# One-hot index tiles built on ScalarE, routing begun between the queries, tile stores on ScalarE's queue, and routing spread over more blocks

## The chip, the cores and the metric

The kernel runs on one core of one Trainium2 chip. The metric is the device time of one launch in microseconds. Below, PE is TensorE, DVE is VectorE, ACT is ScalarE, POOL is GpSimd, and SP is SyncE, which only issues transfers here.

## The reference

Two layers run on 256 tokens and 256 context tokens of width 1024. Each layer has a mixer (four kinds of attention and retention) and then a feed-forward part called PEER, which the change is about. PEER looks up 16 experts per head and token among 16384, by two top-16 lists of 128 keys each:

```python
def one_block(xt):                                   # 128 tokens
    q = (xt @ w_q).reshape(PEER_BLOCK, PEER_HEADS, 2, PEER_DK // 2)
    s = jnp.einsum('thpd,hpkd->thpk', q, keys).astype(jnp.float32)
    s1, i1 = lax.top_k(s[:, :, 0], PEER_TOPK)
    s2, i2 = lax.top_k(s[:, :, 1], PEER_TOPK)
    ...
    top_s, top_pos = lax.top_k(cand, PEER_TOPK)      # cand: all 256 sums of s1 and s2
    eidx = jnp.take_along_axis(cand_idx, top_pos, axis=-1)
    g = jax.nn.softmax(top_s, axis=-1)
    act = jax.nn.gelu(jnp.einsum('td,thkd->thk', xt, u[eidx]).astype(jnp.float32), approximate=False)
    return jnp.einsum('thk,thkd->td', (g * act).astype(xt.dtype), v[eidx])
```

Layer 0 does this for both streams (four tiles of 128 tokens), layer 1 for the 256 tokens alone (two tiles).

## The kernel before, in words

PEER is computed densely for most tiles: the Gelu of *all* 16384 expert rows of `u` with all tokens, times a weight matrix G that is zero except at the chosen experts, times all of `v`. In layer 0 one tile is done sparsely instead (POOL gathers its rows, DVE multiplies them, line 919), three densely; in layer 1 both are dense.

The stages of PEER in a layer are:

1. `qT`: eight query heads, each a product with one 128x1024 block of `wq`, copied by ACT (line 953).
2. `peer_u`: 128 blocks of `u`. For a block SP loads `raw` (three buffers), ACT rounds it to `hi` (line 154), DVE takes the rest as `lo` (line 157; five buffers each of `hi` and `lo`, `NW`), PE does 24 matmuls into a PSUM bank `H` (lines 360 to 362), ACT takes the Gelu into `ast` (line 1145), and every two or four blocks SP stores it to `act_d` (line 1147).
3. `peer_v`: 128 blocks of `v`, for which SP loads G and the stored Gelus back.

Between the blocks of `peer_u` stands the routing of the tiles, as a list of tasks with costs written by hand; it is shared out over the first `P - NT` blocks (`NT` = 16), the rest being the tail, which `peer_v` weaves with its first loads. For a tile the tasks are:

- eight `score` tasks: PE makes the scores of four heads (`scp`, line 980), DVE finds the two top-16 lists by MAX8, FIND_INDEX8 and MATCH_REPLACE8 (lines 985 to 990);
- `lists`, `cand`, the second top-16 and the look-ups, again small DVE operations (lines 1006 to 1060);
- for a dense tile 16 tasks `hot` with their PE part `eight`, here together one "hot". A hot makes G for eight tokens: DVE compares indices with a ramp to get the one-hots `a` (line 1093, 128x2048), multiplies half of them by the weights into `bhl` (line 1095, twice 128x1024), PE multiplies the other half with these (16 small matmuls `gps`, lines 1106 and 1107), ACT copies the result to `gst` (line 1109, twice), and after each second hot SP stores it to `g_d` (line 1112).

A scheduler sets the order within each engine's queue at build time; each engine then works strictly in that order. In the trace `peer_u` of layer 0 runs from about 650 to 1308 us, that of layer 1 from about 2203 to 2609 us. "Hot stretch" below is the time from the first to the 15th hot of a dense tile: three in layer 0, two in layer 1. What lies between two hot stretches is a gap, in which DVE does the scores and lists of the next tile; what lies before the first is the start.

Of the kernel before, what the change touches and what calls it, by code (L numbers as in the profile page):

```python
# [8 lines left out]
F32 = mybir.dt.float32  # L9
F32R = mybir.dt.float32r  # L10
BF = mybir.dt.bfloat16
F16 = mybir.dt.float16
U32 = mybir.dt.uint32
AF = mybir.ActivationFunctionType
OP = mybir.AluOpType
# [4 lines left out]
P = 128  # L20
# [4 lines left out]
NEG = -1e30  # L25
X0 = 256
NW = 5
NT = 16
KEEP = 4
LEAD = 2  # L30
SP = 1
# [82 lines left out]
def hybrid_peer(ctx, tc, resin, cvec, modw, modb, nw, win, uq, uk, uv, colw, nab, retl, gnw,  # L114
                wbr, wo, wq, keys, ub, vb, urow, fnw, consts, rconsts, rope, out):
    nc = tc.nc
    pe, dve, act, pool, sync = nc.tensor, nc.vector, nc.scalar, nc.gpsimd, nc.sync
# [15 lines left out]
    def ps_mm(name="mm"):  # L133
        return ps.tile([P, 512], F32, tag="mm", bufs=3, name=name)
# [25 lines left out]
    def next_w(src, after=None):  # L160
        raw = tb.tile([P, 1024], F32, tag="raw", bufs=3, name="raw")
        sync.dma_start(raw, src)
        return split_w(raw, after)
# [201 lines left out]
    act_d = [dr.tile([64, P, 2, 512 - SP * P], F32, name="act_d"), dr.tile([32, P, 4, 256], F32, name="act_d")]  # L365
    g_d = dr.tile([32, P, P, 16], F32, name="g_d")
# [565 lines left out]
    def peer_u(l, hT, rp, ap_, pre, kp_, normed, xrow, vps):  # L932
# [9 lines left out]
        up2 = rp  # L942
        qT = up2.tile([P, 8, n], F32, name="qT")
        kT = up2.tile([P, 8, P], F32, name="kT")
        sync.dma_start(kT, keys[l])
        for h in range(8):
            if h in pre:
                pt, w = pre[h]
                xt_mm(pt[:, X0:], w, hT, X0, 512)
            else:  # L950
                pt = ps_mm("wq")
                xt_mm(pt[:, :n], next_w(wq[l, h], normed if h in (4, 5) else None), hT, tA, 512)
            act.activation(qT[:, h], pt[:, :n], AF.Copy)
        tasks = []

        def add(cost, f):
# [3 lines left out]
        iota = C["iota"]  # L960
        T = {}

        def route(tt):
# [36 lines left out]
            add(200, lists)  # L1000

            def cand(h4):
                cd = up2.tile([P, 4, 256], F32, tag="cand", bufs=2, name="cand")
                T[tt, "cand"] = cd
                v = v16()[:, h4:h4 + 4]
                dve.tensor_tensor(cd.rearrange("p q (a b) -> p q a b", a=16),
                                  v[:, :, 0, :, None].to_broadcast([P, 4, 16, 16]),
                                  v[:, :, 1, None, :].to_broadcast([P, 4, 16, 16]), op=OP.add)
# [34 lines left out]
            add(1500, weights)  # L1043
            for f in range(2):
                def look(f=f):
                    oh = up2.tile([P, 8, 16, 16], BF, tag="cand", bufs=2, name="oh16")
                    ab = T[tt, "abf"][:, f].rearrange("p (h k) -> p h k", h=8)
                    dve.tensor_tensor(oh, ab[:, :, None, :].to_broadcast([P, 8, 16, 16]),
                                      ib16[:, None].to_broadcast([P, 8, 16, 16]), op=OP.is_equal)
                    o = oh.rearrange("p h a (k c) -> p (h a) k c", c=2)  # L1050
                    iv = T[tt, "if"][:, f].rearrange("p h a c -> p (h a) c")
                    dve.tensor_tensor(o, o, iv[:, :, None, :].to_broadcast([P, P, 8, 2]), op=OP.mult)
                    for m in (8, 4, 2):
                        dve.tensor_tensor(oh[:, :, :m], oh[:, :, :m], oh[:, :, m:2 * m], op=OP.add)
                    dve.tensor_tensor(T[tt, "wn"][:, f].rearrange("p (h k) -> p h k", h=8),
                                      oh[:, :, 0], oh[:, :, 1], op=OP.add)
                add(4000, look)

            def look2():
                if tt not in dense:  # L1060
                    wn = T[tt, "wn"]
                    spw["idx"] = kp_.tile([P, P], U32, name="idx")
                    spw["wgt"] = kp_.tile([P, P], F32, name="wgt")
                    dve.scalar_tensor_tensor(wn[:, 0], wn[:, 0], float(P), wn[:, 1], op0=OP.mult, op1=OP.add)
                    dve.tensor_copy(spw["idx"], wn[:, 0])
                    dve.tensor_copy(spw["wgt"], wn[:, 2])
                    return
                tp = ps_o("idxT")
                for q in range(3):
                    pe.transpose(tp[:, q * P:(q + 1) * P], T[tt, "wn"][:, q], ident)  # L1070
                ix = up2.tile([P, 16, 4, 8], F16, tag="ixT", bufs=2, name="ixT")
                tq = tp[:, :384].rearrange("p (q c t) -> p q c t", q=3, t=8)
                act.activation(ix[:, :, 0], tq[:, 0], AF.Copy)
                act.activation(ix[:, :, 1], tq[:, 1], AF.Copy)
                act.activation(ix[:, :, 2], tq[:, 2], AF.Copy, scale=GS)
                dve.scalar_tensor_tensor(ix[:, :, 3], tq[:, 2], GS, ix[:, :, 2], op0=OP.mult, op1=OP.subtract)
                T[tt, "ix"] = ix
# [3 lines left out]
            for c in range(8):  # L1081
                def gsub(c=c):
                    T[tt, "stage"] = up2.tile([P, P, 16], F32, tag="gst", bufs=2, name="gst")
                add(0, gsub)
                for j in range(2):
                    def hot(c=c, j=j):
                        ix = T[tt, "ix"]
                        cur = [ix[:, c * 2 + j, q:q + 2].rearrange("p q (g t) -> p (q g) t", t=2)[:, :, None, :]
                               .to_broadcast([P, 8, P, 2]) for q in (0, 2)]
                        irep = irep2[:, None].to_broadcast([P, 8, P, 2])  # L1090
                        a = up2.tile([P, 8, P, 2], F16, tag="a12", bufs=2, name="a12")
                        bb = up2.tile([P, 8, P, 2], F16, tag="bhl", bufs=2, name="bhl")
                        dve.tensor_tensor(a, irep, cur[0], op=OP.is_equal)
                        for q in range(2):
                            dve.tensor_tensor(bb[:, q * 4:q * 4 + 4], a[:, :4], cur[1][:, q * 4:q * 4 + 4], op=OP.mult)
                        T[tt, "hot", c, j] = a[:, 4:], bb[:, :4], bb[:, 4:], T[tt, "stage"]

                    def eight(c=c, j=j):
                        a2, bh, bl, stage = T.pop((tt, "hot", c, j))
                        for q in range(2):  # L1100
                            gp = ps_s("gps")
                            for i in range(4):
                                t = q * 4 + i
                                o = gp[:, i * P:(i + 1) * P]
                                at = a2[:, t // 2, :, t % 2]
                                pe.matmul(o, at, bh[:, t // 2, :, t % 2], start=True, stop=False)
                                pe.matmul(o, at, bl[:, t // 2, :, t % 2], start=False, stop=True)
                            tc0 = j * 8 + q * 4
                            act.activation(stage[:, :, tc0:tc0 + 4],
                                           gp.rearrange("p (t i) -> p i t", t=4), AF.Copy)  # L1110
                        if j == 1:
                            sync.dma_start(g_d[tt * 8 + c], stage)

                    add(2800, hot)
                    if "late" in T:
                        add(0, T.pop("late"))
                    T["late"] = eight

        irep2 = up2.tile([P, P, 2], F16, name="irep2")
# [8 lines left out]
        add(0, T.pop("late"))  # L1128
        na = 4 if n == 256 else 2
        total = sum(c for c, _ in tasks)  # L1130
        ti, done = 0, 0.0
        stage, keep = {}, {}
        gen = iter(())

        def block(e):
            w = next_w(ub[l, e])
            pt = ps_mm("H")
            xt_mm(pt[:, :nd], w, hT, tD, 512)
            i, j = divmod(e, na)
            if j == 0:  # L1140
                if is_kept(l, i):
                    stage[0] = keep[i] = kp_.tile([P, na, nd], F32, name=f"keep{i}")
                else:
                    stage[0] = ap_.tile([P, na, nd], F32, tag="ast", bufs=2, name="ast")
            act.activation(stage[0][:, j], pt[:, :nd], AF.Gelu)  # L1145
            if j == na - 1 and i not in keep:
                sync.dma_start(act_d[l][i], stage[0])

        lead = sum(c for c, _ in tasks[:first])
        e0 = 15 if first else 0  # L1150
# [8 lines left out]

        for e in range(P - NT):  # L1160
            if e < e0:
# [7 lines left out]
                continue  # L1169
            share = (e + 1 - e0) / (P - NT - 2.0 - e0)  # L1170
            while ti < len(tasks) and done <= lead + (total - lead) * share:
                c, f = tasks[ti]
# [9 lines left out]
        def tail(i):  # L1182
            for e in range(P - NT + i * NT // 4, P - NT + (i + 1) * NT // 4):
                block(e)
                sparse_step()
# [316 lines left out]
```

## Time and profile before

| | before |
|---|---|
| median of 3 runs | 2960.09 us (2955.0 to 2961.21) |
| profiled execution: own time, span | 2968.41 us, 2966.6 us |
| granted clock, mean | 0.988 of full |
| PE busy | 2876.2 us, 97% |
| DVE busy | 2289.3 us, 77% |
| ACT busy | 1298.6 us, 44% |
| POOL busy | 514.1 us, 17% |
| `hi` on ACT (line 154) | 676 of 1060 ns |
| `lo` on DVE (line 157) | 680 of 1226 ns |

PE is nearly always busy over the span as a whole, and ACT less than half of the time. These are means over the mixer, `peer_u` and `peer_v`, which have different limits; the change touches `peer_u` alone, about 1064 us of the span.

### The profile page before, as it was taken

The page shows a single profiled execution, that of the slowest core. Times are in us where ns is not written, and L with a number is a line of the kernel's source. Part 1 is how long each engine was busy: PE and PEld are TensorE (multiplying, and loading weights), DVE is VectorE, ACT ScalarE, POOL GpSimd, SP SyncE. Part 2 cuts the span into 40 slices and gives each one's busy share as a digit, 9 for nine tenths or more (in the row PEclk, how much of TensorE's full clock was granted, in tenths as well). Part 3 has the DMA queues.
Part 4 walks back from the last instruction along what each step waited for, and adds up shares of the span by engine and source line. Part 5 has one row for each costly group of instructions (what it writes and reads, how often), then busy time and mean ns, then how long its engine had stood idle before and what let it go on. Part 6 is the DMA issues. An engine that isn't in the chain of part 4 may idle for free.

```text
span 2966.6 us, 45423 instructions
## 1 busy us (share of the span) xinstructions
PE 2876.2 (97%) x17323; PEld 2525.1 (85%) x17323; DVE 2289.3 (77%) x3933; ACT 1298.6 (44%) x1907; POOL 514.1 (17%) x378
## 2 busy tenths in 40 slices
PE   8999999998999999999999999999999999999998
PEld 6877767788999999998888888887989999988887
DVE  7778784558999899668888787687668797566666
ACT  7234443543343434333333334455554545544443
POOL 0300111101231323235534340101100000000000
PEclk9999999999999999999999999999999999999999
DMA  7354432536697978999999995564556868888885
GB/s 256 115 161 127 154 99 80 162 114 196 218 344 250 327 280 305 358 388 361 381 371 370 367 333 161 168 214 150 168 174 202 275 200 277 300 297 283 277 274 150
DMA packets 242074, 718.34 MB, mean 242 GB/s; under 512 B 24384, under 2 KB 68544, under 8 KB 236736
## 3 DMA queue, kind: packets, MB, share of 16 engines
q1 hardware_dynamic: 204704, 580.69, 58.0%
q0 software_dynamic: 36864, 134.23, 12.6%
q8 instruction: 135, 2.21, 0.3%
q14 instruction: 83, 0.68, 0.1%
q10 hardware_dynamic: 288, 0.52, 0.0%
HBM read 633.56 MB, written 81.79 MB: 241 GB/s over the span
## 4 chain that ended last, share of the span: by engine, by line
PE 72%; DVE 13%; DMA 8%; ACT 3%; issue 3%; POOL 0%; SPq 0%; ACTq 0%; POOLq 0%; DVEq 0%
PE va L1228 29%; PE H L360 6%; PE H L362 6%; PE H L361 6%; DMA raw<-in_ub_dram 4%; PE proj L360 4%; PE proj L361 4%; PE proj L362 4%; DVE lo L157 3%; DMA mraw<-in_modw_dram 2%; DVE macc L252 2%; DVE gat L919 1%; ACT hi L154 1%; PE sc L466 1%; PE ptp L486 1%
## 5 line engine op out<-in xcount | busy, mean ns | idle before, releaser
L154 ACT ACTIVATE hi<-raw 128x1024 fp32r<-128x1024 f32 x676 | 715.8, 1060 | 1257.7 <-DMA raw<-in_ub_dram 301.0
L157 DVE TENSOR_TENSOR lo<-raw,hi 128x1024 fp32r<-128x1024 f32 x680 | 832.8, 1226 | 505.9 <-ACT hi L154 502.0
L360 PE MATMUL H<-h2h,hi 128*128 128x384 f32 (+1 forms) x2048 | 648.7, 317 | 12.0 <-ACT ast L1145 12.0
L362 PE MATMUL H<-h2h,lo 128*128 128x384 f32 (+1 forms) x2048 | 638.4, 313 | 3.2 <-DVE lo L157 3.2
L361 PE MATMUL H<-h2l,hi 128*128 128x384 f32 (+1 forms) x2048 | 639.1, 312 | 0.0
L360 PEld LDWEIGHTS H<-h2h,hi 128*128 128x128 f32 x2048 | 388.9, 190 | 17.3 <-ACT ast L1145 15.5
L1228 PE MATMUL va<-hi,wh 128*128 128x512 f32 x1280 | 397.9, 389 | 0.4 <-ACT keep L1145 0.4
L1228 PE MATMUL va<-lo,wh 128*128 128x512 f32 x1280 | 397.6, 389 | 0.0
L1228 PE MATMUL va<-hi,wl 128*128 128x512 f32 x1280 | 397.3, 389 | 0.0
L362 PEld LDWEIGHTS H<-h2h,lo 128*128 128x128 f32 x2048 | 388.5, 190 | 5.1 <-DVE lo L157 4.6
L361 PEld LDWEIGHTS H<-h2l,hi 128*128 128x128 f32 x2048 | 389.3, 190 | 0.1
L360 PE MATMUL proj<-hh,hi 128*128 128x256 f32 (+1 forms) x808 | 283.7, 353 | 4.4 <-ACT k_t L555 1.8
L1228 PEld LDWEIGHTS va<-hi,wh 128*128 128x128 f32 x1280 | 240.0, 188 | 50.8 <-ACT keep L1145 0.8
L1228 PEld LDWEIGHTS va<-lo,wh 128*128 128x128 f32 x1280 | 240.3, 188 | 49.9
L1228 PEld LDWEIGHTS va<-hi,wl 128*128 128x128 f32 x1280 | 240.3, 188 | 49.7
L361 PE MATMUL proj<-hl,hi 128*128 128x256 f32 (+1 forms) x808 | 278.0, 345 | 0.5 <-DVE rs L296 0.4
L362 PE MATMUL proj<-hh,lo 128*128 128x256 f32 (+1 forms) x808 | 277.7, 344 | 0.0
L909 POOL DMA_INDIRECT gat<-in_urow_dram,idx x128 | 177.4, 1386 | 518.5 <-DVE gat L919 332.0
L909 POOL DMA_INDIRECT gat<-in_vb_dram,idx x128 | 213.2, 1665 | 268.6 <-DVE spacc L929 247.3
L252 DVE SCALAR_TENSOR_TENSOR macc<-mraw,cs,macc 128x512 f32<-128x512 f32 x224 | 169.3, 792 | 37.7 <-DMA mraw<-in_modw_dram 34.6
L360 PEld LDWEIGHTS proj<-hh,hi 128*128 128x128 f32 x808 | 154.5, 192 | 28.0 <-issue 4.2
L299 POOL TENSOR_TENSOR rs<-rs,mhalf 128x1 f32<-128x1 f32 x16 | 11.0, 687 | 956.6 <-DVE rs L296 919.6
(300 smaller groups left out, 4307.2 us busy)
## 6 DMA issues: line engine op xcount, KB each, us to landing
raw<-in_ub_dram SPq DMA_DIRECT2D x256, 512.0 KB
raw<-in_vb_dram SPq DMA_DIRECT2D x256, 512.0 KB
raw<-in_win_dram SPq DMA_DIRECT2D x112, 512.0 KB
mraw<-in_modw_dram SPq DMA_DIRECT2D x160, 256.0 KB
g_d<-gst SPq DMA_DIRECT2D x40, 1024.0 KB
act_d<-ast SPq DMA_DIRECT2D x64, 384.0 KB
a<-act_d SPq DMA_DIRECT2D x64, 384.0 KB
G<-g_d SPq DMA_DIRECT2D x32, 768.0 KB
```

The lines of the kernel that those rows point to most:

```text
L154: act.activation(hi, raw, AF.Copy)
L157: lo_turn["last"] = dve.tensor_tensor(lo, raw, hi.bitcast(F32), op=OP.subtract)
L252: dve.scalar_tensor_tensor(acc[st], w, cs[:, k, st:st + 1], acc[st], op0=OP.mult, op1=OP.add)
L299: pool.tensor_tensor(r[:, 1:2], r[:, 0:1], mhalf, op=OP.pow)
L360: pe.matmul(o, a, hh[:, k, c0:c1], start=(k == 0), stop=False)
L361: pe.matmul(o, a, hl[:, k, c0:c1], start=False, stop=False)
L362: pe.matmul(o, b, hh[:, k, c0:c1], start=False, stop=(k == KD - 1))
L466: pe.matmul(sps[hb][:, :n], qf(h, tt), kf(h, n), start=True, stop=True)
L486: pe.transpose(tp[:, c * P:(c + 1) * P], pt[:, c * P:(c + 1) * P], ident)
L909: pool.indirect_dma_start(buf[j], None, urow if j < P else vrow, bass.IndirectOffsetOnAxis(ap=idx[:, k:k + 1], axis=0))
L919: dve.scalar_tensor_tensor(g, g, 1.0, xrow, op0=OP.mult, op1=OP.mult, accum_out=hk[:, 0, k:k + 1])
L1228: pe.matmul(pacc[tt][h], x[:, tsl], y[:, h * 512:(h + 1) * 512], start=(e == 0 and x is wh and y is vh), stop=(e == P - 1 and x is wl))
```

## The change

- **One-hots on ACT.** Of a hot's 16 one-hot columns, the eight that are multiplied by weights now come from ACT: eight `Abs` of (ramp minus index) on 128x128 into `dif`, one `Relu` of 1 minus `dif` on 128x1024 into `one`. DVE's compare `a` shrinks from 128x2048 to 128x1024. ACT copies the negated indices once per tile into `nx`. `dif` has one buffer, `one` two.
- **First scores earlier.** Five tasks of the first tile (`begin`, scores of heads 0 to 3) are issued between query heads 0 to 3 and 4 to 7.
- **Stores on ACT's queue.** The 88 `act_d` and 40 `g_d` stores are issued by ACT instead of SP.
- **Longer routing.** `NT` goes from 16 to 12: tasks are spread over the first 116 blocks instead of 112.
- `cand` and `oh16` get one buffer instead of two.

```diff
-NT = 16
+NT = 12
...
-        for h in range(8):
+        def queries(h):
...
+        for h in range(4):
+            queries(h)
         tasks = []
...
-                cd = up2.tile([P, 4, 256], F32, tag="cand", bufs=2, name="cand")
+                cd = up2.tile([P, 4, 256], F32, tag="cand", bufs=1, name="cand")
...
+                T[tt, "nx"] = up2.tile([P, P], F32, tag="nx", bufs=2, name="nx")
+                act.activation(T[tt, "nx"], tp[:, :P], AF.Copy, scale=-1.0)
...
-                        irep = irep2[:, None].to_broadcast([P, 8, P, 2])
-                        a = up2.tile([P, 8, P, 2], F16, tag="a12", bufs=2, name="a12")
+                        irep = irep2[:, None].to_broadcast([P, 4, P, 2])
+                        a = up2.tile([P, 4, P, 2], F16, tag="a2", bufs=2, name="a2")
                         bb = up2.tile([P, 8, P, 2], F16, tag="bhl", bufs=2, name="bhl")
-                        dve.tensor_tensor(a, irep, cur[0], op=OP.is_equal)
+                        dif = up2.tile([P, 4, P, 2], F16, tag="dif", bufs=1, name="dif")
+                        one = up2.tile([P, 4, P, 2], F16, tag="one", bufs=2, name="one")
+                        nx = T[tt, "nx"]
+                        for t in range(8):
+                            x = c * 16 + j * 8 + t
+                            act.activation(dif[:, t // 2, :, t % 2], iota, AF.Abs, bias=nx[:, x:x + 1])
+                        act.activation(one, dif, AF.Relu, scale=-1.0, bias=1.0)
+                        dve.tensor_tensor(a, irep, cur[0][:, 4:], op=OP.is_equal)
                         for q in range(2):
-                            dve.tensor_tensor(bb[:, q * 4:q * 4 + 4], a[:, :4], cur[1][:, q * 4:q * 4 + 4], op=OP.mult)
-                        T[tt, "hot", c, j] = a[:, 4:], bb[:, :4], bb[:, 4:], T[tt, "stage"]
+                            dve.tensor_tensor(bb[:, q * 4:q * 4 + 4], one, cur[1][:, q * 4:q * 4 + 4], op=OP.mult)
+                        T[tt, "hot", c, j] = a, bb[:, :4], bb[:, 4:], T[tt, "stage"]
...
-                            sync.dma_start(g_d[tt * 8 + c], stage)
+                            act.dma_start(g_d[tt * 8 + c], stage)
...
-        ti, done = 0, 0.0
+        ti, done = 5, 0.0
+        for c, f in tasks[:ti]:
+            f()
+            done += c
+        for h in range(4, 8):
+            queries(h)
...
-                sync.dma_start(act_d[l][i], stage[0])
+                act.dma_start(act_d[l][i], stage[0])
```

The scheduler orders the queues anew. On ACT, at the first hots of layer 0's first dense tile, the order before is:

```order
L1075 ACTIVATE ixT<-idxT 128x16x8
L154 ACTIVATE hi<-raw 128x1024
L1145 ACTIVATE ast<-H 128x384
L154 ACTIVATE hi<-raw 128x1024
L1145 ACTIVATE ast<-H 128x384
L1109 ACTIVATE gst<-gps 128x128x4 x2
L154 ACTIVATE hi<-raw 128x1024
L1145 ACTIVATE ast<-H 128x384
L1109 ACTIVATE gst<-gps 128x128x4 x2
L154 ACTIVATE hi<-raw 128x1024
```

and of the change, at the same place (lines 1104 and 1105 are the new `Abs` and `Relu`, 1122 is `gst`, 1163 `ast`):

```order
L1081 ACTIVATE ixT<-idxT 128x16x8
L1104 ACTIVATE dif<-consts,nx 128x128 x8
L154 ACTIVATE hi<-raw 128x1024
L1105 ACTIVATE one<-dif 128x1024
L1163 ACTIVATE ast<-H 128x384
L1104 ACTIVATE dif<-consts,nx 128x128 x8
L1165 DMA act_d<-ast 128x768
L1105 ACTIVATE one<-dif 128x1024
L1122 ACTIVATE gst<-gps 128x128x4 x2
L1104 ACTIVATE dif<-consts,nx 128x128 x8
L1163 ACTIVATE ast<-H 128x384
L1105 ACTIVATE one<-dif 128x1024
```

Nine new instructions stand in each hot, and the stores stand among `hi`, `ast` and `gst`.

On DVE, in the same hot stretch, the order before is:

```order
L1093 TENSOR_TENSOR a_7296<-irep_5723,ixT 128x2048
L157 TENSOR_TENSOR lo<-raw,hi 128x1024
L1095 TENSOR_TENSOR bhl<-a_7296,ixT 128x1024 x2
L919 SCALAR_TENSOR_TENSOR gat,hk<-gat,xrow 128x1024
L157 TENSOR_TENSOR lo<-raw,hi 128x1024
L1093 TENSOR_TENSOR a_7358<-irep_5723,ixT 128x2048
```

and of the change (989 to 994 are the scores of the next tile):

```order
L1106 TENSOR_TENSOR a_7320<-irep_5595,ixT 128x1024
L989 MAX v_8380<-scp_8382 128x8
L990 MAX_INDEX i_8381<-v_8380,scp_8382 128x8
L1108 TENSOR_TENSOR bhl<-one,ixT 128x1024 x2
L992 MATCH_REPLACE rep<-v_8380,scp_8382 128x128
L989 MAX v_8380<-scp_8382 128x8
L993 MAX v_8380<-rep 128x8
L990 MAX_INDEX i_8381<-v_8380,scp_8382 128x8
L994 MAX_INDEX i_8381<-v_8380,rep 128x8
L1106 TENSOR_TENSOR a_7429<-irep_5595,ixT 128x1024
L1108 TENSOR_TENSOR bhl<-one,ixT 128x1024 x2
```

Before, the next tile's scores stood behind the hots; now about 140 small operations for the next tile stand among the hots of the first hot stretch of each layer.

On PE, within layer 0's fifth query, the eight `scp` matmuls of the first four heads (line 980 before, 984 now) are moved ahead:

```order
 L361 MATMUL wq<-h2l,hi 128x512
 L362 MATMUL wq<-h2h,lo 128x512
+L984 MATMUL scp_5601<-kT,qT 128x128
+L984 MATMUL scp_5602<-kT,qT 128x128
+L984 MATMUL scp_5601<-kT,qT 128x128
+L984 MATMUL scp_5602<-kT,qT 128x128
+L984 MATMUL scp_5601<-kT,qT 128x128
+L984 MATMUL scp_5602<-kT,qT 128x128
 L360 MATMUL wq<-h2h,hi 128x512
```

Before, they stood behind the last matmul of the eighth query. On SP the stores are gone, and 119 loads of `raw` stand in a row where at most a few stood between two stores.

## Rows read from the trace of the kernel before

**Rows 1.** Windows: start:end, length, PE, PEld, DVE, ACT, POOL busy (count), clock, DMA share, GB/s.

```profile
650.20:812.60 162.40, 149.73 (x848) 145.40 (x845) 150.25 (x506) 52.87 (x74) 28.03 (x22) 0.96 0.60 196
812.60:892.10 79.50, 74.95 (x562) 72.37 (x560) 74.14 (x106) 34.98 (x57) 25.09 (x18) 0.98 0.93 338
892.10:975.90 83.80, 81.31 (x487) 78.47 (x484) 81.51 (x256) 28.92 (x45) 17.09 (x15) 1.00 0.73 256
975.90:1061.40 85.50, 81.41 (x594) 78.39 (x591) 78.68 (x137) 36.63 (x60) 26.77 (x18) 0.96 0.92 334
1061.40:1145.60 84.20, 78.66 (x461) 76.42 (x458) 84.15 (x236) 29.04 (x42) 27.75 (x18) 0.98 0.75 261
1145.60:1225.90 80.30, 75.87 (x564) 73.45 (x562) 72.97 (x96) 35.80 (x60) 28.70 (x20) 0.96 0.95 350
1225.90:1308.20 82.30, 81.64 (x474) 80.94 (x473) 49.83 (x64) 30.47 (x45) 25.30 (x20) 1.00 0.97 373
2202.70:2292.10 89.40, 86.50 (x736) 85.23 (x732) 81.52 (x249) 43.20 (x66) 0.00 (x0) 1.00 0.64 200
2292.10:2377.20 85.10, 85.10 (x827) 84.44 (x824) 66.89 (x70) 46.94 (x79) 0.00 (x0) 1.00 0.79 268
2377.20:2467.80 90.60, 90.58 (x791) 89.85 (x789) 83.13 (x251) 45.13 (x71) 0.00 (x0) 1.00 0.65 203
2467.80:2552.80 85.00, 85.00 (x827) 84.37 (x825) 66.41 (x70) 46.60 (x79) 0.00 (x0) 1.00 0.85 289
2552.80:2608.70 55.90, 55.90 (x476) 55.82 (x474) 25.27 (x23) 27.77 (x43) 0.00 (x0) 1.00 0.91 306
```

**Rows 2.** The same stretches, matmuls, weight loads and Gelus of `H` alone.

```profile
892.10:975.90 83.80, 74.28 (x409) 71.45 (x409) 8.60 (x18) 1.00 0.73 256
2377.20:2467.80 90.60, 86.83 (x721) 85.88 (x722) 10.94 (x30) 1.00 0.65 203
```

**Rows 3.** A wait of PE in `peer_u` of layer 0: us in total, times, longest.

```profile
PE H L360 <- ACT ast L1145: 11.2, 7, 4.1
```

**Rows 4.** Chain of waits from 829 to 848 us, DVE's links.

```profile
829.68 1.14 DVE a L1093
830.82 1.14 DVE lo L157
831.95 1.22 DVE bhl L1095 x2
846.29 1.14 DVE gat L919 x2
```

**Rows 5.** ACT's operations: timeline at 870 us, chain at 64 us, and one tile.

```profile
870.64 1.06 ACT L154 ACTIVATE hi<-raw 128x1024 fp32r<-128x1024 f32 x1
871.61 0.47 ACT L1145 ACTIVATE ast<-H 128x384 f32<-128x384 f32 x1
871.98 1.08 ACT L1109 ACTIVATE gst<-gps 128x512 f32<-128x512 f32 x2
63.97 1.17 ACT dec L542 x4
L542 ACT ACTIVATE dec<-rcon,lg x16: 386/388/402, 61.9 to 1855.8; 128x128 f32<-128x128 f32 x16
```

**Rows 6.** The start of layer 0: fourth query on ACT, first score, last waited-for scores.

```profile
627.63 0.58 ACT L953 ACTIVATE qT<-wq 128x512 f32<-128x512 f32 x1
651.30 0.49 DVE L985 MAX8 v<-scp 128x8 f32<-128x128 f32 x2
738.40 2.07 PE L980 MATMUL scp<-kT,qT 64*128 64x128 f32 x8 [7.95 <-DVE rep L988]
```

**Rows 7.** The `act_d` stores on SP, and SP's and ACT's waits (650 to 1308 us).

```profile
L1147 SPq DMA_DIRECT2D act_d<-ast x88: 320/326/2327, 660.3 to 2599.6; - x88
SPq L1147 <- ACT ast L1145: 204.4, 54, 9.5
ACT hi L154 <- DMA raw<-in_ub_dram: 226.2, 70, 10.5
```

More of the change, by code (lines that the diff above doesn't have):

```diff
@@ L1045, in look @@
                 def look(f=f):
-                    oh = up2.tile([P, 8, 16, 16], BF, tag="cand", bufs=2, name="oh16")
+                    oh = up2.tile([P, 8, 16, 16], BF, tag="cand", bufs=1, name="oh16")
                     ab = T[tt, "abf"][:, f].rearrange("p (h k) -> p h k", h=8)
```

## The prediction

> **What bounds the kernel now.** I read the windows first, cut at the first and the 15th hot of each dense tile [rows 1]. Layer 0's `peer_u` is 658.0 us long, its PE is busy for 623.6: the idle 34.4 us are 12.7 in the start, 4.1 to 4.6 in each hot stretch, 2.5 and 5.5 in the gaps, 0.7 in the tail. DVE is full in the gaps (81.51 of 83.80, 84.15 of 84.20) and nearly so in the hot stretches; ACT is at 35 to 37 us of 80. Layer 1's 406.0 us hold 403.1 of PE: 2.9 idle, all in the start. So PE's work, which the change keeps, allows at most some 37 us of gain, and layer 1 has almost none to give. Then the waits: PE waits in layer 0 for `ast`, which empties its banks, 11.2 us in seven waits [rows 3], and 8.0 us once for a score bank that DVE still reads [rows 6]. The chain through a hot stretch alternates between PE and DVE's `a`, `lo`, `bhl` and `gat` at 1.14 to 1.22 us each [rows 4].
>
> **Prices.** DVE pays 1.14 for `lo` and `gat`, 1.14 for `a` and 1.22 for the two `bhl` [rows 4]. The halved `a` is a `bhl` in size: 0.60. A hot thus falls from 2.36 to 1.82, over 80 hots 43 us. Of the 81.51 us in the first gap, 15 `lo`, 16 `gat` and two hots take 40.0; the other 41.5 are 137 small operations, 0.30 each. On ACT `hi` takes 0.97 to the next start, `ast` 0.37, `gst` 0.54 [rows 5]. A `Relu` is as large as `hi`: 1.06. `Abs` on 128x128 with a pointer operand is not in the trace; the nearest is `dec` (line 542) on the same shape, four in 1.17 us, 0.29 each. From above 0.39 bounds it, the duration of one `dec` without overlap; from below 0.13, a quarter of a 512-column `gst`. I take 0.29, as it runs eight in a row. A store costs its queue 0.33 [rows 7]. ACT's part in a hot goes from 1.08 to 1.08 + 8 x 0.29 + 1.06 = 4.5 us, over 80 hots 270 us.
>
> A block of `u` costs PE 74.28/17 = 4.37 us in layer 0, 86.83/30 = 2.89 in layer 1 [rows 2] and a hot 0.94 (what 25 blocks of 2.89 leave of 85.1, in 14 hots). Longer routing moves blocks: I counted in the orders how many stand in each stretch after the change. Before has 32, 14, 17, 15, 17, 14, 19 in layer 0, the change 32.5, 13.5, 19, 14, 19, 15, 15; layer 1 has 29, 25, 30, 25, 19, then 31, 24, 33, 24, 16. Each stretch below is compared with its time of before for the changed number of blocks, at 4.28 us (just under the tail's 81.64/19 = 4.30 [rows 1]) and 2.89; both counts sum to 128, so this price cancels.
>
> **Layer 0.**
> - *Start, 164.5 before.* The fourth query is copied at 627.6, so the first score can begin at 629 instead of 651.3 [rows 6]: 22.3 us earlier. DVE then has six more `lo` and three more `gat` between first score and first hot, 10.3 us. The first hot comes 12 us earlier, after 150.4 us; PE was busy for 149.7 of this stretch, so all of its idle 12.7 goes and there is no more to gain. **-14.1.**
> - *First hot stretch, 77.4 before.* DVE's queue holds 14 hots (25.5), 12 `lo` and 13 `gat` (28.5) and 142 small operations of the next tile (43): **97**, where it was busy for 74. ACT has 112 `Abs`, 14 `Relu`, 28 `gst`, 12 `hi`, 14 `ast`, 14 stores: 32.5 + 14.8 + 15.1 + 11.6 + 5.2 + 4.6 = 84. PE has 73. The queue is in order, so the hots wait behind the scores. **+19.6.** Bounds: 80, if the five buffered `lo` keep PE fed while DVE runs late, and 101, if ACT's 84 does not lie beside it fully.
> - *First gap, 92.4 before.* DVE now has 76 us, PE 19 blocks and a little (83 + 2): 85. **-7.4.**
> - *Second hot stretch, 81.2 before.* PE 75.5, DVE up to 78, ACT 83 by the same sum. PE's idle was 4 in such a stretch, so between 79.5 and 88; I take ACT's 83. **+1.8.**
> - *Second gap, 92.8 before.* DVE falls to 60, since its work was done early; PE 84.5. **-8.3.**
> - *Third hot stretch, 84.6 before.* ACT 85, PE 78: 84. **-0.6.**
> - *Tail, 65.2 before for 15 blocks.* The last `g_d` store and the loads of G now fall into fewer blocks. The DMA share was 0.97 of 82.3; less four blocks of 0.5 MB at 373 GB/s it still needs 74. I take 68, between PE's 65 and this. **+2.8.**
>
> Sum: **-6.2**, from 658 to 652.
>
> **Layer 1.** Start, 95.2 before: I take 1 of the 2.9 idle: 94. First hot stretch, 82.2 before: DVE 14 hots, 22 `lo` and 140 small operations, 25.5 + 25.1 + 42.4 = 93; ACT 95 with 24 `hi` and 24 `ast` of 0.26; PE 83. Two engines at 93 to 95 in strict orders, with no sparse step between: 97 (85 to 101). Gap, 99.3 before: PE 33 blocks and 2: 97. Second hot stretch, 82.1 before: PE 83, ACT 82: 84.5. Tail, 47.2 before for 16 blocks: 51, since the same loads of G come in fewer blocks. Sum **+17.5**: 406 to 423.5. Here no idle PE pays for it: DVE's 43 us were not on the path, ACT's 270 come onto it.
>
> **Stores and buffers.** I price the move of the stores at nothing beyond ACT's 0.33 each. SP waited 204.4 us for `ast` with a store at its head, and ACT 226.2 us for `raw` behind it [rows 7]: it looks as if `raw` would come much earlier. But what counts is PE, and it waited 11.2 us for `ast` [rows 3]; a store that no longer blocks SP can give at most that. The Trainium skill (DMA: Bandwidth & Descriptors, "Issuing engines are not separate DMA queues") says that transfers issued by any engine run on the same 16 DMA engines and interleave, so issuing from another saves only the sequencer's time; by that rule the move takes 128 x 0.33 = 42 us off SP and puts it on ACT, and the loads themselves come no faster; the trace bears it out so far that ACT's 226.2 us of waiting cost PE only 11.2. What waits behind a store on ACT is `hi` and `ast` of the next block; the store follows the `ast` or `gst` that it needs, so its wait is done when it comes up. One `cand` buffer costs nothing: the two uses are in order on DVE.
>
> **Sum.** -6.2 + 17.5 = **+11.3 us** against the profiled execution, whose own time is 2968.4, 8 above the median of the runs; mixer and `peer_v` keep their order. On the median 2960.1: **2971 us**. Its own range is 2966 to 2995: the first hot stretches' bounds give -17 -12 and +4 +4, the tail +6, the others up to +5 each, of which not all fall together; the low end is cut where other cases begin.
>
> **Rivals.**
> 1. *The buffers absorb it: faster.* In both first hot stretches five `hi`/`lo` are ready ahead, 5 x 4.37 = 22 us of PE work in layer 0, 14 in layer 1. If DVE's lateness of 97 - 73 = 24 stays within them and is paid back in the gap (DVE 76 of 85), these stretches are 80 and 86: -17 and -11, and with 4 less in the others 2971 - 32 = 2939. For it: DVE lags PE only within a stretch. Against it: in the hot stretches before, five buffers did not prevent 4 to 5 us of idle with DVE less full, and the gap pays back 9. It decides at a first stretch under about 86 in layer 0.
> 2. *`Abs` does not overlap.* At 0.39 each ACT has 95 in every hot stretch: +11 in the three that ACT sets, +3 in the others, and `hi` comes late, so SP's loads too, which now all stand in a row on three buffers: 2971 + 39 = 3010. For it: `dif` has one buffer, so that `Abs` of the next hot waits for `Relu`. Against it: `dec` ran at 0.29 four times in a row.
> 3. *It cancels.* The start and gaps give 30 us in layer 0; if layer 1's stretch loses only 7 instead of 15 and the tails nothing, the sum is -3: 2957, no difference.
>
> **Chances.** Differences under 0.2% (6 us) are about what a measurement of this kernel cannot tell from none. My forecast (6 to 35 slower) 0.36, rival 2 0.15, cancelling 0.20, rival 1 0.29. So faster 0.29, same 0.20, slower 0.51. For 8 in 10 the range reaches from rival 1's time to rival 2's: 2938 to 3010; below it some of rival 1 is left out, above it some of rival 2.
>
> **What would show it.** The start is right if the first score begins near 629, the 8.0 us wait at line 980 is gone, and the first hot comes near 800. The first hot stretches are right if DVE is over 95% busy there and they are 95 to 100 long; if they are under 86, rival 1 is. ACT's price is right if an `Abs` starts every 0.29 us and ACT sums to 82 to 85 in the hot stretches; rival 2, if it is 95 and PE waits for `ast` and `gst`. The gaps are right if DVE is idle in them and PE is not. The forecast is wrong above all if DVE's work for the next tile, though earlier in the queue, gets done while PE lives from its buffers.

## The result, and the profile after

The change takes 3122.52 us (median of 4 runs, 3114.23 to 3127.66) against 2960.22: a ratio of 1.0543, 95% interval 1.0526 to 1.056. The forecast was 2971, with a range from 2938 to 3010. The sign was right; the size was wrong by an order of magnitude.

The profiled execution has a span of 3112.3 us, 145.7 more than before. On its page PE is busy for 2924.0 us, 47.8 more, though it does the same matmuls; the other 97.9 us are idle time of PE. All of it lies in `peer_u`: from the first to the last `H` matmul layer 0 takes 734.8 us (657.8 before) and layer 1 477.2 (405.8).

The windows of the changed kernel, cut at the same events as [rows 1] (start:end, length, PE, PEld, DVE, ACT, POOL busy, clock, DMA share, GB/s):

```profile
645.20:801.40 156.20, 149.84 (x860) 146.47 (x859) 136.93 (x419) 59.40 (x92) 28.46 (x24) 0.98 0.66 219
801.40:911.10 109.70, 86.08 (x589) 80.46 (x586) 99.06 (x298) 77.45 (x176) 17.01 (x13) 0.88 0.61 212
911.10:1003.50 92.40, 85.69 (x494) 84.84 (x492) 79.18 (x174) 44.64 (x76) 32.33 (x25) 0.94 0.87 310
1003.50:1115.70 112.20, 87.83 (x585) 81.36 (x583) 78.58 (x189) 76.12 (x173) 14.48 (x12) 0.85 0.59 203
1115.70:1203.20 87.50, 84.23 (x493) 83.38 (x491) 58.58 (x80) 44.84 (x78) 30.34 (x24) 0.98 0.91 333
1203.20:1306.30 103.10, 88.65 (x591) 82.66 (x589) 59.01 (x85) 81.23 (x184) 18.77 (x14) 0.88 0.63 221
1306.30:1380.20 73.90, 67.02 (x381) 66.02 (x379) 45.54 (x59) 29.19 (x40) 24.50 (x18) 0.95 0.99 376
2273.30:2364.60 91.30, 91.15 (x781) 90.64 (x780) 77.91 (x209) 51.05 (x90) 0.00 (x0) 1.00 0.67 208
2364.60:2486.10 121.50, 100.18 (x838) 95.55 (x835) 97.33 (x275) 87.37 (x195) 0.00 (x0) 0.89 0.52 174
2486.10:2585.70 99.60, 96.81 (x829) 96.16 (x827) 50.98 (x49) 71.09 (x131) 0.00 (x0) 1.00 0.73 238
2585.70:2693.20 107.50, 91.90 (x804) 88.52 (x802) 48.68 (x60) 76.72 (x169) 0.00 (x0) 0.94 0.57 196
2693.20:2750.70 57.50, 50.62 (x404) 49.79 (x402) 26.24 (x24) 29.86 (x45) 0.00 (x0) 0.94 0.83 276
```

The loss sits in the five hot stretches: 109.7, 112.2, 103.1, 121.5 and 107.5 us where 97, 83, 84, 97 and 84.5 were forecast, 108.5 us in excess. No engine is full in them. ACT's sums, 76 to 87, are near the forecast ones, but ACT is idle for 22 to 36 us in each: lengths less busy time give 32.3, 36.1, 21.9, 34.1 and 30.8. The third and fifth stretch have no next-tile work on DVE (59.01 and 48.68 busy) and are long all the same. The granted clock is 0.85 to 0.94.

What ACT and PE wait for, first ACT in the first hot stretch (us in total, times, longest), then PE over the whole span, then SP:

```profile
ACT ast L1163 <- PE H L362: 30.1, 12, 8.7
...
PE H L360 <- ACT hi L154: 55.0, 29, 6.6
PE H L362 <- DVE lo L157: 45.7, 32, 6.1
...
SPq L162 <- DVE lo L157: 460.5, 79, 37.2
```

ACT waits for PE and PE for ACT. The third row, of SP from 801 to 1307 us, rules out late loads: for 460.5 us SP waited for `lo` to free a `raw` buffer, so `raw` lay there and `hi` was late. One such place, on ACT's timeline (start, length, what):

```profile
873.98 0.49 ACT L1163 ACTIVATE ast<-H 128x384 f32<-128x384 f32 x1 [1.27 <-PE H L362]
874.37 1.05 ACT L1105 ACTIVATE one<-dif 128x1024 f16<-128x1024 f16 x1
874.51 0.33 ACTq L1165 DMA_DIRECT2D act_d<-ast  x1
875.32 1.08 ACT L1122 ACTIVATE gst<-gps 128x512 f32<-128x512 f32 x2
876.27 0.45 ACT L1104 ACTIVATE dif<-consts,nx 128x128 f16<-128x128 f32 x1
876.42 0.33 ACTq L1125 DMA_DIRECT2D g_d<-gst  x1
876.80 2.19 ACT L1104 ACTIVATE dif<-consts,nx 128x128 f16<-128x128 f32 x7
878.86 1.04 ACT L154 ACTIVATE hi<-raw 128x1024 fp32r<-128x1024 f32 x1
```

and what PE and DVE make of it:

```profile
879.95 0.44 PE L360 MATMUL H<-h2h,hi 128*128 128x384 f32 x1 [1.55 <-ACT hi L154]
880.23 0.34 PE L361 MATMUL H<-h2l,hi 128*128 128x384 f32 x1
886.68 0.69 PE L362 MATMUL H<-h2h,lo 128*128 128x384 f32 x1 [6.11 <-DVE lo L157]
...
885.40 1.22 DVE L157 TENSOR_TENSOR lo<-raw,hi 128x1024 fp32r<-128x1024 f32 x1
```

The `hi` of the next block stands *behind* the `ast` of the block that PE is just finishing. So ACT waits for PE; then it does `one`, two `gst` and eight `dif`, 4.9 us after the start of `ast`, before it makes `hi`; then DVE, busy with the next tile, makes `lo` 5.5 us later; and only then can PE go on. Call the number of blocks by which ACT's queue holds `hi` ahead of `ast` the **lead**. Counted from ACT's order, it is 2 to 5 in all hot stretches before. In those of the change it is 0 to 2 after the first few blocks, and 0 at 28 of 92 blocks. Call a block with lead 0 a **place**.

Counted in the trace by blocks, these 28 places hold nearly the whole loss. Between the end of such a block and the end of the next one on PE lie 11.7 us in the mean, with 2.6 us of other ACT work between `ast` and `hi`; behind the other 64 blocks it is 4.0 us. (Some hots stand there too: 1.5 behind a place, 0.6 behind another block, by the forecast under 1 us each.) PE is idle for 112.0 us behind the 28 places and for 2.8 behind the other 64, of 132.4 in the two `peer_u`. In run e5 below, where the lead is 3, the 83 blocks of the hot stretches take 4.6 us each, with 12.9 us of idle time together.

### The profile page after: what moved, and what is told of

It is laid out like the page before. It is cut to its first block, busy times and chain, and to the rows that moved or that the text cites. A ratio compares the mean times of both kernels' runs of the same rounds, so it can differ in the third digit from the quotient of the medians.

```text
span 3112.3 us, 46158 instructions
## 1 busy us (share of the span) xinstructions
PE 2924.0 (94%) x17323; PEld 2561.6 (82%) x17323; DVE 2256.2 (72%) x3933; ACT 1568.2 (50%) x2632; POOL 523.1 (17%) x378
## 4 chain that ended last, share of the span: by engine, by line
PE 69%; DVE 14%; issue 6%; DMA 4%; ACT 4%; POOL 1%; SPq 0%; POOLq 0%; DVEq 0%; ACTq 0%
PE va L1246 28%; PE H L362 6%; PE H L360 6%; PE H L361 6%; DVE lo L157 4%; PE proj L360 4%; PE proj L362 3%; PE proj L361 3%; DMA mraw<-in_modw_dram 1%; ACT hi L154 1%; DVE macc L252 1%; PE sc L466 1%; PE attno L499 1%; POOL gat L909 1%; PE ptp L486 1%
## 5 line engine op out<-in xcount | busy, mean ns | idle before, releaser
L360 PE MATMUL H<-h2h,hi 128*128 128x384 f32 (+1 forms) x2048 | 663.7, 324 | 59.1 <-ACT hi L154 55.0
L362 PE MATMUL H<-h2h,lo 128*128 128x384 f32 (+1 forms) x2048 | 660.8, 323 | 45.7 <-DVE lo L157 45.7
L361 PE MATMUL H<-h2l,hi 128*128 128x384 f32 (+1 forms) x2048 | 655.0, 320 | 0.0
L360 PEld LDWEIGHTS H<-h2h,hi 128*128 128x128 f32 x2048 | 405.2, 198 | 66.9 <-ACT hi L154 61.0
L362 PEld LDWEIGHTS H<-h2h,lo 128*128 128x128 f32 x2048 | 403.8, 197 | 56.0 <-DVE lo L157 55.7
L361 PEld LDWEIGHTS H<-h2l,hi 128*128 128x128 f32 x2048 | 404.3, 197 | 0.1
L909 POOL DMA_INDIRECT gat<-in_vb_dram,idx x128 | 232.2, 1814 | 247.0 <-DVE spacc L929 231.7
L909 POOL DMA_INDIRECT gat<-in_urow_dram,idx x128 | 165.0, 1289 | 611.5 <-DVE gat L919 404.7
L1104 ACT ACTIVATE dif<-consts,nx 128x128 f16<-128x128 f32 x640 | 209.3, 436 | 1.7
L1163 ACT ACTIVATE ast<-H 128x384 f32<-128x384 f32 (+1 forms) x224 | 97.7, 436 | 171.5 <-PE H L362 170.1
```

The costliest lines, as they stand in the source:

```text
L360: pe.matmul(o, a, hh[:, k, c0:c1], start=(k == 0), stop=False)
L361: pe.matmul(o, a, hl[:, k, c0:c1], start=False, stop=False)
L362: pe.matmul(o, b, hh[:, k, c0:c1], start=False, stop=(k == KD - 1))
L909: pool.indirect_dma_start(buf[j], None, urow if j < P else vrow, bass.IndirectOffsetOnAxis(ap=idx[:, k:k + 1], axis=0))
L1104: act.activation(dif[:, t // 2, :, t % 2], iota, AF.Abs, bias=nx[:, x:x + 1])
```

## The experiments

All ratios are to the kernel before, timed on the same chip (medians there 2963 to 2965 us for the runs, 2960 for the change), with 95% intervals. "ACT one-hots" is the number of columns per hot that ACT builds.

| run | ACT one-hots | stores on | lead in hot stretches | next-tile work among hots on DVE | us | ratio |
|---|---|---|---|---|---|---|
| the change | 8 | ACT | mostly 0 to 2 | 142, 79, 0; 140, 0 operations | 3122.5 | 1.0543 (1.0526 to 1.0560) |
| e1 | none | ACT | 2 to 5 | 7 at most | 2947.2 | 0.9935 (0.9918 to 0.9952) |
| e2 | 8 | SP | mostly 1 | 48, 65, 0; 68, 0 | 2990.0 | 1.0080 (1.0064 to 1.0097) |
| e3 | 8 | SP | mostly 1 | 46, 28, 0; 41, 0 | 2987.9 | 1.0075 (1.0058 to 1.0092) |
| e4 | 8 | ACT | 3 | 143, 79, 0; 137, 0 | 3037.6 | 1.0247 (1.0230 to 1.0264) |
| e5 | 8 | ACT | 3 | none | 3000.0 | 1.0122 (1.0105 to 1.0139) |
| e6 | 8 | ACT | 0 to 2 | none | 3127.0 | 1.0556 (1.0536 to 1.0576) |
| e7 | 8 | SP | 3 to 4 | 57, 13, 0; 0, 0 | 2983.5 | 1.0068 (1.0051 to 1.0085) |
| e8 | none | ACT | 3 to 5 | 9 at most | 2956.8 | 0.9979 (0.9964 to 0.9994) |
| e10 | 4 | SP | 3 to 5 | none | 2944.4 | 0.9933 (0.9910 to 0.9956) |
| e11 | none | ACT | 3 to 5 | none | 2947.8 | 0.9945 (0.9925 to 0.9964) |
| e12 | none | SP | 2 to 5 | 9 at most | 2952.0 | 0.9959 (0.9944 to 0.9974) |
| e15 | 4 | ACT | 3 to 4 | 48, 28, 0; 0, 0 | 2970.5 | 1.0019 (1.0008 to 1.0030) |
| e16 | 4 | ACT | 3 to 4 | none | 2968.2 | 1.0014 (1.0002 to 1.0025) |

The semicolon parts layer 0's three hot stretches from layer 1's two. Runs e9, e13 and e14 force places of lead 0 and stand below.

**e1, the change without ACT's one-hots.** DVE's old lines 1093 and 1095 are put back, `nx`, `dif` and `one` are gone.

> The change without ACT's one-hots: DVE compares all 2048 columns again; early scores, stores on ACT's queue, longer routing stay. Theory A (ACT's queue holds hi only 0 to 2 blocks ahead of ast in the hot stretches, so that ACT waits for PE with the next hi behind it, and PE for ACT): here the queue holds hi 3 or more ahead throughout, so 2950 us (2930 to 2970), PE's waits for hi under 5 us. Theory B (ACT's added work is too much in itself, whatever the order): also 2950. Theory C (stores on ACT's queue hold up hi): 3100 (3070 to 3125).

2947.2 us. The rest of the change is a gain of 0.65%; A and B hold, C falls as stated (the lead is 2 to 5, where A had 3 or more).

**e2, the one-hots alone,** in the kernel before.

> The kernel before with ACT's one-hots alone (and one cand buffer). The queue holds hi 1 to 2 blocks ahead of ast in the hot stretches. Theory A: 3100 us (3060 to 3140), hot stretches over 100 us. Theory B: 3110 (3090 to 3140). Theory C: 2970 (2950 to 2990).

2990.0, at the upper end of C's range. The one-hots alone cost 0.8%, not 5%. A's claim that a lead of 1 is enough to lose the time is refuted here, and so is B.

**e3, the stores back on SP.**

```diff
-                            act.dma_start(g_d[tt * 8 + c], stage)
+                            sync.dma_start(g_d[tt * 8 + c], stage)
...
-                act.dma_start(act_d[l][i], stage[0])
+                sync.dma_start(act_d[l][i], stage[0])
```

> The change with the stores back on SP. The queue holds hi 1 block ahead of ast in most of the hot stretches (0 to 2 in the change). Theory A: 3090 us (3050 to 3125), a little less than the change since a lead of 0 is rare. Theory B: 3110 to 3120, less the 128 issues of 0.33 us at most. Theory C: 2970 (2950 to 3000).

2987.9: again in C's range, 135 us below the change. So most of the loss needs both, ACT's one-hots *and* the stores on ACT's queue; e1 has one and e3 the other. But moving them also lets the scheduler order the queues anew: the lead is 1 instead of 0, and 46 operations instead of 142 stand among the first tile's hots. Whether the stores or the order cost the time was to be told next.

**e4, `hi` and `lo` written three blocks ahead,** stores on ACT.

```diff
+AHEAD = 3
...
+        ws = []
...
+        def fetch(e):
+            while len(ws) < min(e + AHEAD, P):
+                ws.append(next_w(ub[l, len(ws)]))
...
-            w = next_w(ub[l, e])
+            fetch(e + 1)
+            w = ws[e]
...
         for e in range(P - NT):
+            fetch(e)
```

> The change with the load, hi and lo of a block written three blocks ahead in the program, so that ACT's queue holds hi 3 blocks ahead of ast in all hot stretches; the work of each engine is the same. Theory A: 2975 us (2940 to 3010), PE's waits for hi and lo under 20 us, hot stretches 85 to 97 us. Theory B: 3100 (3080 to 3130), hot stretches still over 100. Theory C: 3100 too.

3037.6: between both. The third and fifth hot stretch fell from 103.1 and 107.5 to 85.2 and 89.2 us, as A said; those with next-tile work stayed at 109.4, 107.7 and 120.5. There `gst` waited for PE, and PE for `bhl` and `lo`, which stood behind that work on DVE (busy 98.53 of 109.40 in the first). PE's waits over the span, of which A had put those for `hi` and `lo` under 20 us:

```profile
PE H L363 <- DVE lo L158: 36.5, 19, 4.0
PE gps L1120 <- DVE bhl L1109: 21.8, 9, 5.3
```

**e5, e4 and the next tile's scores queued behind the last hot; e6, these scores alone.**

```diff
+                    with tc.issue_after(inst(T["bhl"])) if "bhl" in T else ExitStack():
                         for f in range(2):
...
-                            dve.tensor_tensor(bb[:, q * 4:q * 4 + 4], one, cur[1][:, q * 4:q * 4 + 4], op=OP.mult)
+                            T["bhl"] = dve.tensor_tensor(bb[:, q * 4:q * 4 + 4], one, cur[1][:, q * 4:q * 4 + 4], op=OP.mult)
```

> The change with hi and lo three blocks ahead as before, and the scores of the next tile queued on DVE behind the last hot of the tile before; the stores stay on ACT's queue. Theory O (the order is what costs: next-tile work among the hots on DVE, and hi 0 to 2 blocks ahead on ACT; the scheduler made this order because the stores were on ACT): 2985 us (2965 to 3005), hot stretches as long as ACT's sum, 76 to 83 us in layer 0 and 88 to 92 in layer 1. Theory P (the stores themselves hold up ACT's queue): 3030 (3015 to 3060).

> The change with only the scores queued behind the last hot; hi stays 0 to 2 blocks ahead in the hot stretches, stores on ACT. Theory O: 3060 us (3030 to 3090): all five hot stretches at 100 to 108 us, like the third and fifth of the change, which have no next-tile work in them. Theory P: 3100 or more (3090 to 3130). If next-tile work alone were the cause: 2985.

e5 takes 3000.0, as O said and P did not. e6 takes 3127.0: above O's range and inside P's, so neither theory holds as it was stated. O was wrong that next-tile work costs time where the lead is 0 to 2; P is wrong that the stores explain the loss by themselves, since e5 has them too. Between the two edits only the three blocks ahead differ (`raw`, `hi` and `lo`), with the same stores and the same work on each engine: **127 us for the lead**. In the traces `peer_u` is 137 us shorter, and the stretch between the layers 11 longer. The next-tile work is worth 38 us where the lead is 3 (e4 against e5) and nothing where it is 0 to 2 (the change against e6). The windows of the five hot stretches, e5's and then e6's:

```profile
806.80:883.10 76.30, 72.60 (x554) 65.20 (x551) 54.12 (x79) 75.50 (x177) 14.87 (x13) 1.00 0.80 280
988.10:1062.80 74.70, 71.69 (x534) 65.47 (x532) 54.86 (x80) 74.15 (x172) 14.24 (x12) 0.98 0.85 291
1168.50:1243.70 75.20, 68.78 (x525) 62.41 (x522) 55.03 (x80) 74.69 (x177) 14.66 (x13) 1.00 0.82 282
2312.80:2402.90 90.10, 90.10 (x868) 88.58 (x864) 54.90 (x67) 88.00 (x198) 0.00 (x0) 1.00 0.71 240
2503.30:2590.60 87.30, 87.30 (x842) 86.37 (x840) 53.74 (x65) 86.79 (x195) 0.00 (x0) 1.00 0.75 252
...
804.20:905.30 101.10, 87.49 (x588) 81.79 (x586) 61.96 (x101) 81.44 (x185) 19.99 (x15) 0.88 0.70 237
1004.50:1112.30 107.80, 88.99 (x570) 82.38 (x568) 58.83 (x95) 80.22 (x183) 16.22 (x14) 0.87 0.67 222
1212.70:1311.60 98.90, 84.67 (x570) 78.77 (x568) 60.22 (x87) 80.89 (x184) 19.91 (x15) 0.88 0.70 241
2370.90:2486.70 115.80, 98.96 (x826) 95.00 (x824) 52.28 (x64) 87.63 (x196) 0.00 (x0) 0.88 0.56 187
2596.10:2708.70 112.60, 92.63 (x804) 88.65 (x801) 51.88 (x63) 87.67 (x195) 0.00 (x0) 0.94 0.59 197
```

In e5 ACT does what it did in the changed kernel, in 75 to 90 us, and is idle for 2.1 at most. In layer 0 its sum now sets the stretch, as the prediction took it to; in layer 1 PE is full as well (90.10 of 90.10 and 87.30 of 87.30). In e6 ACT has about the same sums and is idle for 18 to 28 us in each.

PE's waits in e6, for comparison with the two rows of the change above:

```profile
PE H L360 <- ACT hi L154: 73.7, 33, 6.7
PE H L362 <- DVE lo L157: 25.0, 38, 2.9
```

**e7, e4 with the stores on SP; e8, the stores alone in the kernel before.**

> The change with hi and lo three blocks ahead and the stores on SP; the scheduler then leaves at most 57 next-tile operations among a tile's hots, against 143. Theory O and theory P both: 2980 us (2960 to 2995), as with the stores on SP alone (2988), the hot stretches being as long as ACT's sum.

> The kernel before with only the stores moved to ACT's queue. Theory O: no harm where ACT has idle time and the order keeps hi 3 or more blocks ahead: 2960 us (2945 to 2968 with before at 2965). Theory P: slower by 20 to 60 us, 2985 to 3025.

2983.5, which both theories gave and which decides nothing between them, and 2956.8, as O said and P did not. The hot stretches of e7 are ACT's nearly from end to end (73 to 87 us of its work in 73 to 89); the first:

```profile
813.60:888.80 75.20, 74.88 (x562) 66.15 (x560) 66.89 (x168) 75.20 (x180) 15.93 (x12) 1.00 0.79 280
```

**e9, no part of the change, but every eighth `hi` put behind the `ast` of the block before it.**

```diff
+            late = e % 8 == 4 and e > 4
+            with tc.issue_after(inst(T["ast"])) if late else ExitStack():
-            w = next_w(ub[l, e])
+                w = next_w(ub[l, e])
```

> The kernel before, without any part of the change, but with hi of every eighth block queued on ACT behind the Gelu (ast) of the block before it: 29 or so places where the queue holds hi no block ahead. Theory O (lead): each place costs PE ast 0.47 + hi 1.06 + lo 1.22 = 2.7 us and some more for the clock, 29 x 3 to 4.5 = 87 to 130: 3050 to 3095 us. If the lead is harmless and only ACT's added work counts: 2964 to 2975.

3001.9 us (1.0131, 1.0104 to 1.0158): 37 us in a kernel that has nothing else of the change. The edit makes 30 places, 15 in each layer, so 1.2 us each, less than half of the low bound. Nothing stands between `ast` and `hi` at these places, where 2.6 us did in the change; PE is idle for 32 us behind the 30. But the rest of the order changed too: 44, 41, 0; 112, 0 next-tile operations stand among the hots, where before has 9 at most. So not all of the 37 us need be the lead's.

**e13 and e14, the same places in e7 and e10:** is it that ACT was full?

> The kernel of e7 (ACT builds eight columns, hi three ahead, stores on SP; ACT busy for 99 to 100% of the hot stretches), with hi of every eighth block queued behind the Gelu of the block before it, as in e9. Theory R (where ACT is full, each wait of ACT for PE adds its whole length to the stretch): more than e9's 37 us over e7, since some 10 of the 29 places lie in hot stretches and cost 4 us or more there: 3055 us (3035 to 3080). If the places cost the same whatever ACT's load: 3020 (3012 to 3030).

> The kernel of e10 (four columns on ACT; ACT busy for 80% of the hot stretches) with the same places. Theory R: ACT has room, so the places cost as in e9: 2944 + 37 = 2981 us (2970 to 2993). If ACT's work itself, full or not, makes the places dear: 3000 or more.

3033.8 (1.0242, 1.0217 to 1.0268), 50 over e7 and between the two ranges on record, and 3025.6 (1.0209, 1.0185 to 1.0232), 81 over e10 and in the range for "ACT's work itself". Theory R falls: ACT with room pays more. What a place costs is not fixed, and how full ACT is does not order it. That ACT's work makes the places dear is not shown either, since the scheduler made a new order in each of these runs: 47, 85, 0; 131, 0 next-tile operations stand among e13's hots and 35, 55, 0; 135, 0 among e14's, against 57 at most in e7 and none in e10. At the places `lo` begins 0.8 us after the end of its `hi` in e9, 1.4 in e13 and 1.9 in e14, the order of the three costs. This points to DVE's queue, but no run holds that queue fixed.

**e10, four columns on ACT, four on DVE;** hi ahead, stores on SP.

```diff
-                        a = up2.tile([P, 4, P, 2], F16, tag="a2", bufs=2, name="a2")
+                        a = up2.tile([P, 6, P, 2], F16, tag="a2", bufs=2, name="a2")
...
-                        for t in range(8):
+                        for t in range(4):
```

> ACT builds four columns of a hot instead of eight, DVE the other four; hi three blocks ahead, stores on SP. If what was left of the loss there (2983 us with eight columns) is ACT's sum in the hot stretches: ACT's part of a hot falls by 4 x 0.29 + 0.5 = 1.7 us, 24 us in each stretch, so that PE bounds them: 2955 us (2940 to 2968). If it is something else, DVE's order say: 2980 (2972 to 2990).

2944.4, 39 below e7, as the forecast for ACT's sum had it. ACT is at 56 to 57 of 68 to 71 us in layer 0's hot stretches, and layer 1's are at PE's 85.1 and 85.0 again.

**e11, e1 with hi ahead; e12, the early scores alone.**

> The change without ACT's one-hots, and hi and lo three blocks ahead. By theory O nothing is to be had, since hi was 3 or more ahead there too: 2946 us (2938 to 2956), as without it (2947).

> The kernel before with the first four heads' scores between the queries alone. If the first score's 22 us come through to the first hot in part, 2955 us (2948 to 2961 with before at 2964); the rest of the 18 us by which the change without one-hots is faster would then be the stores' 7 and the longer routing's few. If the start is bound by PE and not by DVE: 2964.

2947.8 and 2952.0. Where the lead is 2 to 5 already, writing `hi` further ahead gives nothing. The early scores give 12 of e1's 18 us, the stores 7 by e8; the longer routing was not run by itself.

**e15 and e16, e10 with the stores on ACT,** e16 with the scores behind the last hot.

> The kernel of e10 with the stores on ACT's queue. If the stores cost nothing where ACT has room and the order keeps hi three ahead: 2946 us (2938 to 2958). If the stores as such delay ACT: 2965 or more.

> The kernel of e15 (four columns on ACT, hi three ahead, stores on ACT) with the next tile's scores queued behind the last hot, so that DVE's queue holds no next-tile work among the hots, as with the stores on SP (e10, 2944). If that next-tile work is what made e15 26 us longer than e10: 2950 us (2940 to 2958). If stores on ACT's queue cost as such: 2965 or more, as in e15 (2970).

2970.5 and 2968.2: 26 and 24 us over e10. Both lie where the texts on record had put them if stores on ACT cost as such, and the next-tile work does not explain it. What the traces say of it stands under "Open" below.

## Why the prediction was wrong

**What failed** is the step that sums each engine's work in a hot stretch and takes the largest sum, first with "PE has 73. The queue is in order, so the hots wait behind the scores", then "I take ACT's 83". The sums were near: ACT 77.45, 76.12 and 81.23 against 84, 83 and 85, in layer 1 87.37 and 76.72 against 95 and 82, an `Abs` every 0.29 us (seven in 2.06 above). Of the 84, 4.6 were stores; in the rows above the store at 874.51 is issued while `one` runs, so that it took no time from ACT's other work. (PE's price of a hot, 0.94, comes to 0.92 by its own numbers; nothing hangs on it.) So what failed is the overlap, not a price: the step lets three engines work side by side without asking whether they can. What stood in the orders and was not read is which instruction stands before which. Sums bound a stretch only if each engine has something to do while it waits; with the lead at 0 ACT and PE take turns, 112 us of idle PE behind 28 places. In the change the stretches are ACT's sum and 22 to 36 us of waiting. e5 and e7, with the lead at 3, are what the step described.

**The stores,** priced "at nothing beyond ACT's 0.33 each", were the second failure: 135 us by e3. The argument that a store's wait is over when it comes up holds in the change: ACT is idle for `ast <- PE`, not for a store. With the stores moved the scheduler came to another order. In e5 and e6, with the stores on ACT in both, the lead is worth 127 us, so a lead like e6's can account for the 135. Without the one-hots the move gives 0.2% (e8). The Trainium skill (DMA: Bandwidth & Descriptors, "Issuing engines are not separate DMA queues") has it that issuing from several engines saves only the sequencer's time, and e8's 0.2% doesn't contradict that. It says nothing of what else moves.

**The rivals.** The second named part of it (`hi` late, while ACT is filled) but with the wrong cause: `Abs` does overlap, and `raw` was not late. The first, that buffers absorb it, needs a lead that the queue didn't have.

**What held.** The first score came at 623.4 instead of 651.3, the first hot at 801.4 where "near 800" stood, and e12 shows the early scores alone. The start itself took 156.2 us instead of 150.4, but `peer_u` began 5 us earlier. DVE fell in the second gap to 58.58 (60). The 8.0 us wait at the score bank shrank to 2.5. The gaps were 92.4 and 87.5 for 85 and 84.5, the tails 73.9 and 57.5 for 68 and 51, layer 1's start and gap 91.3 and 99.6 for 94 and 97: 23 us too low together. And the core of the forecast, that ACT's work comes onto the path in layer 1 and costs more than DVE's relief gives, is what e2, e3 and e7 show in their traces. Against before, `peer_u` of layer 0 and of layer 1 changed by +6.5 and +18.4, +1.4 and +13.5, -7.1 and +9.5 us, where -6.2 and +17.5 were forecast. It is a small part of the change's 162 us, though: that the sign came out right there is mostly due to the lead, which the forecast did not have. The whole runs e2, e3 and e7 are at +25, +23 and +20; 10 us of e3's and 13 of e7's lie between the two `peer_u`, which the prediction took as unchanged and which the change itself left so. Why that stretch grows in some runs is not known.

**Open.** Why the scheduler drops the lead to 0 with the stores on ACT can't be told from a trace. What one place without lead costs is not settled (1.2 us in e9, 1.7 in e13, 2.7 in e14, by 30 places each). So is why four columns with the stores on ACT are 24 us slower than on SP (e16 against e10), when with no one-hots they are 7 us faster: the order differs there too (lead 3 to 4 against 3 to 5), and a run with one order and both queues was not made. By the traces 8.5 us of it lie in layer 0's `peer_u`, 10.1 in layer 1's and 8.9 between them; one wait that e10 doesn't have is ACT's for an `act_d` store to land before it can fill `ast` again, 9.4 us in two waits. With eight columns and a lead of about 3 the stores on ACT are 17 us slower too (e5 against e7). That they cost something of their own where ACT also makes one-hots is thus not ruled out; it is small beside the 127 us.

## What to carry to other kernels

Before adding work to an engine that feeds the bound engine, count in its new order how many blocks ahead the feeding instruction stands of the one that waits for the bound engine; if that reaches 0, sums of busy time no longer bound the time. Writing the feeding work some blocks ahead in the program holds the lead (127 us here), and moving a store to another queue can change it. Of all versions, four columns on ACT with the lead held and the stores on SP (e10, 2944.4 us) and no one-hots on ACT (e1, 2947.2) are some 0.7% faster than before, and can't be told apart.

## What the hardware showed

Waiting cost PE twice. At the place shown above, the windows of PE's wait, the 4 us after it and what follows are:

```profile
880.60:886.60 6.00, 0.00 (x0) 0.00 (x0) 6.00 (x25) 6.00 (x14) 0.00 (x0) 0.50 0.00 0
886.70:890.70 4.00, 4.00 (x13) 4.00 (x14) 4.00 (x14) 0.29 (x1) 0.94 (x1) 0.50 0.45 131
891.00:892.80 1.80, 1.80 (x12) 1.69 (x10) 1.80 (x3) 0.10 (x1) 0.00 (x0) 1.00 0.81 266
```

The granted clock was 0.50 (1.2 GHz) in the wait and for 4 us of work after it, with a matmul every 0.32 us, then 1.00 (2.4 GHz) and one every 0.17. Over the hot stretches that makes 0.85 to 0.94. Counted from the trace's clock record, PE worked at 0.50 for 107.0 us behind the 28 places and for 0.1 us behind the other 64 hot blocks. Over the span it is 138.3 us in the change against 56.3 before; half of the 82.0 more is 41 of the 47.8 us for which PE is busy longer with the same matmuls. The prediction had no term for it.
